# Hybrid decoder trunk on one core: the scan layer's cross product in rounded halves, its first tile's scaling issued earlier, and other PSUM banks for two products of the attention

## The chip, the cores and the metric

The kernel runs on one core of one Trainium2 chip. The metric is the device time of one execution in microseconds (us). TensorE (PE; PEld is its loading of the stationary operand) multiplies matrices into PSUM, VectorE (DVE) and ScalarE (ACT) work on tiles of 128 partitions, GpSimd (POOL) does small arithmetic and issues some DMAs, and SyncE (SP) issues the rest. Each engine takes its instructions in one fixed order, and semaphores make it wait for the others.

## The reference

The program is a decoder trunk of two layers on a sequence of 256 tokens with 1024 features, everything in float32. Each layer is a SwiGLU block, a mixer and a second SwiGLU block, each followed by a layer norm. The mixer of the first layer is a sparse attention: an indexer chooses 64 keys for each query, and 16 heads attend to them over a latent of 256 values. The mixer of the second layer is a state-space scan with 32 heads of 64 features in 4 groups. The parts that the change touches are these, cut from the reference:

```python
# attention: logits, softmax, and the values behind them (per head h)
p = softmax(einsum('bthr,btkr->bthk', q_abs, c_sel) * scale + mask)
o = einsum('bthr,hrd->bthd', einsum('bthk,btkr->bthr', p, c_sel), w_uv)

# scan: two chunks of 128 tokens; the second gets what the first left as its state
xdt = x * dt[..., None]
y_diag = einsum('bcgrls,bcsgrp->bclgrp', cb[:, :, :, None] * decay, xdt)
states = einsum('bclgn,bclgrp->bcgrpn', bm, xdt * decay_to_end[..., None])
y_off = einsum('bclgn,bcgrpn->bclgrp', cm, prev) * exp(a_cs_l)[..., None]
yz = (y_diag + y_off + x * d_skip) * silu(z)
yz = yz * rsqrt(mean(square(yz), -1) + eps)    # per group of 512 features
out = (yz * norm_g) @ w_out
```

For two chunks, `y_off` of the second chunk is (C of chunk 1, times B of chunk 0) applied to the first chunk's `xdt * decay_to_end`. The matrix C·B between the chunks is the "cross" of the kernel.

## The kernel before

**Products in halves.** A plain float32 matmul runs in two passes on the traced PE. Nearly all products of the kernel are done another way: each operand is split into a rounded part H (type float32r, written by a copy on ACT) and the rest L = x − H (a subtraction on DVE), and `mm3` (lines 538 to 541) issues three matmuls, H·H, H·L and L·H. Weights come as 128 x 1024 blocks over SP's DMA queue (`raw`), ACT makes `wh` from each (line 326, or 324 with a scale), DVE makes `wl` (lines 354 and 351), and for five blocks ACT writes −raw and a POOL DMA adds (lines 332 and 333). `W.pump` makes the next blocks' halves, ahead of their use.

**The order.** Every instruction is issued in the order of the Python code, and that order is the order on each engine; no scheduler changes it. Tiles live in rotating pools; of PSUM's eight banks, two are called `pmm`, two `ptr`, and four `acc00`, `acc01`, `acc10`, `acc11`. `pspare(n)` (line 453) deals out `pmm`, `pmm`, `acc00`, `acc01` (n = 2) in turn, by the counter `spare[0]`.

**The attention's stretch.** `logits(0, 1, 0)` computes 8 heads' logits of the first 128 queries into two spare banks; DVE adds the mask (line 1202) and ACT takes the exponentials (line 1213). Then `v_half` runs three times: two blocks' product on PE into a spare bank, and a copy to SBUF on ACT (line 1174). Then `out_both(0, 0)` multiplies the first block of the output weights into `acc00` and `acc01`.

**The scan's groups.** The loop at line 1676 handles four groups g of eight heads. The two chunks of tokens are called tiles 0 and 1. Between the group's own steps it puts pieces of other work, f[0] to f[7], to keep PE fed: for g = 0 and 1 projections of the next group (`xs_tile`: 24 matmuls on PE, then a convolution, one instruction on ACT at line 1497 and three on DVE at line 1500; `z_half`), for g = 2 the last projections in turn with pieces of the output product (`out_piece`), for g = 3 output pieces. The order in a group is: f[0]; `x_tok` (or, for g = 0, `decay_cb`); `x_end`, which makes `xe` on DVE; f[1]; f[2]; `diag(0)`, 8 small products on PE; `gate(0)` on DVE; `carry`, one float32 product of `cross` and `xe` on PE (line 1587) with two DVE steps; f[3]; `square(0)` on ACT (line 1597) and `root(0)` on POOL (lines 525 and 531); `diag(1)` and `gate(1)`; f[4]; `square(1)`, `root(1)`, then `norm(0)` on ACT (line 1603); f[5]; `y_tr(0)`, four transposes on PE of what `norm(0)` wrote (line 1608), split into halves `yH`, `yL`; and the same for tile 1. What `cross` holds is computed once, ahead of the loop (line 1522).

Of the kernel before, what the change touches and what calls it, by code (L numbers as in the profile page):

```python
# [11 lines left out]
F32 = mybir.dt.float32  # L12
F32R = mybir.dt.float32r
# [399 lines left out]
def trunk_kernel(ctx: ExitStack, tc: tile.TileContext, widths, forms, x, ln_g, ln_b, wts, kvg, convp,  # L413
                 dt_bias, a_log, d_skip, norm_g, out):
    nc = tc.nc
# [3 lines left out]
    wk = ctx.enter_context(tc.tile_pool(name="wk", bufs=1))  # L419
# [6 lines left out]
    def nm(s):  # L426
        cnt[0] += 1
        return f"{s}_{cnt[0]}"
# [4 lines left out]
    def f2(s):  # L433
        return wk.tile([128, 512], F32, name=nm(s), tag="f2", bufs=9)
# [4 lines left out]
    def r2(s):  # L439
        return wk.tile([128, 512], F32R, name=nm(s), tag="r2", bufs=10)  # L440

    def tiny(s, n=32):
        return wk.tile([128, n], F32, name=nm(s), tag=f"tiny{n}", bufs=14 if n == 32 else 4)
# [7 lines left out]
    spare = [0]  # L451

    def pspare(n):

        spare[0] = (spare[0] + 1) % (n + 2)
        if spare[0] < 2:
            return pmm()
        a, b = divmod(spare[0] - 2, 2)
        return psum.tile([128, 512], F32, name=nm("psp"), tag=f"acc{a}{b}", bufs=1)
# [74 lines left out]
    def split_psum(H, L, ps):  # L534
        nc.scalar.copy(H, ps)
        nc.vector.tensor_sub(L, ps, H.bitcast(F32))  # L536

    def mm3(ps, lh, ll, rh, rl, first, last, on=False):
        nc.tensor.matmul(ps, lh, rh, start=first, stop=False, skip_group_check=on)  # L539
        nc.tensor.matmul(ps, lh, rl, start=False, stop=False, skip_group_check=on)  # L540
        nc.tensor.matmul(ps, ll, rh, start=False, stop=last, skip_group_check=on)  # L541
# [474 lines left out]
    def attention(xT, u, ln_i):  # L1016
# [3 lines left out]
        lt, ki, qs, ss = {}, {}, {}, {}  # L1020
# [157 lines left out]
        oT, po, lgs, pTs = {}, {}, {}, {}  # L1178

        def pair_heads(t, hf, b):  # L1180
            return head_banks(8, 512 // (128 * (t + 1)), 8 * hf)[2 * b:2 * b + 2]

        def logits(t, hf, b, now=True):

            hss = pair_heads(t, hf, b)
            nk, per = 128 * (t + 1), len(hss[0])
            bank = pmm if t else lambda: pspare(2)
            ps = [bank(), bank()]
            for i in range(per):
                for q in range(2):  # L1190
                    h = hss[q][i]
                    p0, hp = (h % 2) * 64, h // 2
                    nc.tensor.matmul(ps[q][:, i * nk:(i + 1) * nk],
                                     qv[hp // 4][p0:p0 + 64, hp % 4, t * 128:(t + 1) * 128],
                                     kT[hp // 4][p0:p0 + 64, (hp % 4) * 256:(hp % 4) * 256 + nk],
                                     start=True, stop=True)
            mx = tiny("mx")
            lgs[t, hf, b] = lg = [f2("lg"), f2("lg")]
            for q in range(2):
                for i, h in enumerate(hss[q]):  # L1200
                    c = slice(i * nk, (i + 1) * nk)
                    nc.vector.tensor_tensor_reduce(out=lg[q][:, c], in0=ps[q][:, c], in1=mb[t][:, :nk],
                                                   scale=-(HD ** -0.5), scalar=3e38, op0=ALU.add, op1=ALU.min,
                                                   accum_out=mx[:, h:h + 1])
                if now:
                    exps(t, hss[q], lg[q], mx)
            return lambda: [exps(t, hss[q], lg[q], mx) for q in range(2)]

        def exps(t, hs, lg, mx):
            nk = 128 * (t + 1)  # L1210
            for i, h in enumerate(hs):
                c = slice(i * nk, (i + 1) * nk)
                nc.scalar.activation(lg[:, c], lg[:, c], AF.Exp, bias=mx[:, h:h + 1], scale=-1.0,
                                     accum_out=sums[t][:, h:h + 1])
# [22 lines left out]
        def pv(t, hf, b):  # L1237

            hss = pair_heads(t, hf, b)
            if not b:  # L1240
                po[t, hf] = psum.tile([128, 512], F32, name=nm("po"), tag=f"acc1{hf}", bufs=1)
            pT = pTs.pop((t, hf, b))
            for i in range(len(hss[0])):
                for kt in range(t + 1):
                    for q in range(2):
                        h = hss[q][i]
                        p0, j = (h % 2) * 64, h % 8 // 2
                        nc.tensor.matmul(po[t, hf][p0:p0 + 64, j * 128:(j + 1) * 128], v[kt][:, h * 64:(h + 1) * 64],
                                         pT[q][:, (i * (t + 1) + kt) * 128:(i * (t + 1) + kt + 1) * 128],
                                         start=kt == 0, stop=kt == t)  # L1250

        def o_split(t, hf):
            oT[t, hf] = (r2("oH"), r2("oL"))
            split_psum(*oT[t, hf], po[t, hf])
# [42 lines left out]
        k_pair(3)  # L1297
        pv(0, 0, 0)
        o_split(0, 0)
        logits(0, 1, 0)  # L1300
        for i in range(2):
            W.free(uk + i)
# [74 lines left out]
    def ssd(xT, u, ln_i):  # L1377
# [132 lines left out]
            W.pump(1 + i % 2)  # L1510

        cbm = f4("cbm")
        cross = f2("cross")

        def cb_cross():

            pt = pspare(4)
            for g in range(SG):
                c = slice(g * 256 + 128, g * 256 + 256)
                nc.tensor.matmul(pt[:, g * 128:(g + 1) * 128], bT[:, g * 256:g * 256 + 128], cTt[:, c],  # L1520
                                 start=True, stop=True)
            nc.scalar.copy(cross, pt)

        def cb(t):
            pt = pspare(4)
# [9 lines left out]
        def hv(ap):  # L1535
            return ap.rearrange("p (h d) -> p h d", h=8)

        def hb(ap, g):
            return ap[:, g * 8:(g + 1) * 8][:, :, None].to_broadcast([128, 8, 64])
# [13 lines left out]
                                 .to_broadcast([128, 8, 128]))  # L1553

        yT = {}
        y, xd, xe, ss = {}, {}, {}, {}

        def x_tok(t, g):

# [12 lines left out]
        def x_end(g):  # L1572
            xe[g] = f2("xe")
            nc.vector.tensor_mul(hv(xe[g]), hv(y[0]), hb(dend, g))

        def diag(t, g):
            m = M.pop((t, g))
# [6 lines left out]
        def carry(g):  # L1584

            po = ptr()
            nc.tensor.matmul(po, cross[:, g * 128:(g + 1) * 128], xe[g], start=True, stop=True)
            nc.vector.tensor_mul(hv(xe[g]), hv(po), hb(eacs, g))
            nc.vector.tensor_add(xd[1], xd[1], xe[g])

# [4 lines left out]
        def square(t):  # L1595
            ss[t] = tiny("ss")
            nc.scalar.activation(xd[t], y[t], AF.Square, accum_out=ss[t][:, 0:1])
# [4 lines left out]
        def norm(t):  # L1602
            nc.scalar.activation(y[t], y[t], AF.Copy, scale=ss[t])
# [72 lines left out]
        for g in range(SG):  # L1676
            if g < 2:
                f = [lambda i=i: xs_tile(g + 1, i, u + i) for i in range(4)]
                f += [lambda t=t, i=i: (z_half(g + 2, t, i, u + 4), W.pump(1)) for t in range(2) for i in range(2)]
            elif g == 2:  # L1680
                x3 = [lambda i=i: xs_tile(3, i, u + 2 * i) for i in range(4)]
                o0 = [lambda i=i: out_piece(i, u + 2 * i + 1) for i in range(4)]
                f = [x3[0], x3[1], o0[0], x3[2], o0[1], x3[3], o0[2], o0[3]]
            else:
                f = [lambda i=i: out_piece(4 + i, u + i) for i in range(6)]
            f[0]()
            if g:
                x_tok(0, g)
                x_tok(1, g)
            else:  # L1690
                decay_cb(0, 0)
                decay_cb(1, 0)
            x_end(g)
            f[1]()
            f[2]()
            py[0] = diag(0, g)
            gate(0, g, py[0])
            carry(g)
            if g < 3:
                decay_load(0, g + 1)  # L1700
            f[3]()
            square(0)
            root(0)
            py[1] = diag(1, g)
            gate(1, g, py[1])
            if g < 3:
                decay_load(1, g + 1)
            f[4]()
            square(1)
            root(1)  # L1710
            norm(0)
            if g < 3:
                decay_seg(0, g + 1)
            f[5]()
            y_tr(0, g)
            norm(1)
            if g < 3:
                decay_seg(1, g + 1)
                f[6]()
                flush()  # L1720
                y_tr(1, g)
                decay_exp(0, g + 1)
                decay_exp(1, g + 1)
                f[7]()
                decay_cb(0, g + 1)
                decay_cb(1, g + 1)
                W.lows()
                u += 8
# [19 lines left out]
    u, _ = ffn(xT, u, 5, last=True)  # L1748
# [36 lines left out]
```

## Time and profile before

| | us |
|---|---|
| median of 3 runs (lowest, highest) | 1011.57 (1011.35, 1012.05) |
| the profiled execution's own time | 1011.34 |
| its span from the first to the last instruction | 1009.6 |
| PE busy, sum of the records | 998.8 |
| DVE busy | 905.6 |
| ACT busy | 662.0 |
| POOL busy | 109.5 |

The execution that was profiled is one of its own; 1.7 us of its time lie outside the span. [...] A start is a start; an end of a matmul is modelled. The page's chain and its "idle before" name what an engine waited for last.

### The profile page before, as it was taken

The numbers are of one execution on the slowest core, as the hardware profiler recorded it, in microseconds if no ns is written. First come the engines' busy times: TensorE is split into PE (matmuls) and PEld (weight loads), VectorE is DVE, ScalarE is ACT, GpSimd is POOL, SyncE is SP. The second block draws the span as 40 slices with busy tenths as digits, with TensorE's granted clock in tenths as the row PEclk, the third lists the DMA queues.
The fourth block names the chain that finished last, engine by engine and source line by source line (L and its number), as shares of the span: only waits on it lengthen the run. The fifth ranks groups of instructions, "written<-read, shape, count | busy, mean of one in ns | idle before, by whom it ended". The sixth has DMA issues, their size and how long they took to land.

```text
span 1009.6 us, 14555 instructions
## 1 busy us (share of the span) xinstructions
PE 998.8 (99%) x5273; PEld 845.8 (84%) x5273; DVE 905.6 (90%) x1224; ACT 662.0 (66%) x968; POOL 109.5 (11%) x149
## 2 busy tenths in 40 slices
PE   9999999999999999999999999999999999999997
PEld 6888888898788888888888888999899888888886
DVE  6899999889898999999899998788999978899996
ACT  6676776476755777764576776486876645676670
POOL 0010110100000101100010110150221100010100
PEclk9999999999999999999999999999999999999999
DMA  9699889551654899995599989557765654699981
GB/s 346 221 289 282 241 260 344 181 172 59 232 181 127 272 275 239 264 376 202 126 276 271 248 264 359 172 171 248 220 211 182 243 188 136 169 261 288 289 254 42
DMA packets 66055, 231.69 MB, mean 229 GB/s; under 512 B 8112, under 2 KB 9136, under 8 KB 65984
## 3 DMA queue, kind: packets, MB, share of 16 engines
q1 hardware_dynamic: 54288, 189.84, 51.6%
q0 software_dynamic: 11120, 40.41, 21.7%
q8 instruction: 41, 0.67, 0.3%
q10 hardware_dynamic: 576, 0.52, 0.2%
q14 instruction: 30, 0.25, 0.1%
HBM read 193.48 MB, written 1.08 MB: 193 GB/s over the span
## 4 chain that ended last, share of the span: by engine, by line
PE 91%; DVE 5%; DMA 1%; ACT 1%; issue 1%; POOL 0%; ACTq 0%; DVEq 0%; POOLq 0%
PE pmm L539 13%; PE pmm L540 13%; PE pmm L541 13%; PE acc L539 10%; PE acc L541 10%; PE acc L540 10%; PE ptr L539 2%; PE ptr L541 2%; PE ptr L540 2%; PE pxs L539 2%; PE pxs L541 2%; PE pxs L540 2%; PE pmm L705 1%; DVE wl L354 1%; PE ptr L705 1%; PE ptr L795 1%
## 5 line engine op out<-in xcount | busy, mean ns | idle before, releaser
L354 DVE TENSOR_TENSOR wl<-raw,wh 128x1024 fp32r<-128x1024 f32 (+3 forms) x424 | 495.9, 1212 | 14.9 <-ACT wh L326 14.3
L326 ACT CAST wh<-raw 128x1024 fp32r<-128x1024 f32 (+2 forms) x431 | 429.0, 1043 | 97.0 <-DVE raw L293 47.3
L539 PE MATMUL acc<-wh,hH 128*128 128x512 f32 (+1 forms) x352 | 138.1, 392 | 0.0
L541 PE MATMUL acc<-wh,hL 128*128 128x512 f32 (+1 forms) x352 | 136.6, 388 | 0.0
L540 PE MATMUL acc<-wl,hH 128*128 128x512 f32 (+1 forms) x352 | 136.3, 387 | 0.0
L539 PE MATMUL pmm<-wh,xT 128*128 128x512 f32 (+2 forms) x304 | 119.1, 392 | 0.0
L541 PE MATMUL pmm<-wh,xT 128*128 128x512 f32 (+2 forms) x304 | 116.8, 384 | 0.0
L540 PE MATMUL pmm<-wl,xT 128*128 128x512 f32 (+2 forms) x304 | 116.7, 384 | 0.1
L266 POOL DMA_DIRECT2D raw<-raw x64 | 55.7, 875 | 490.6 <-DVE raw L293 260.5
L541 PE MATMUL pmm<-wh,xf 128*128 128x512 f32 x256 | 99.6, 389 | 0.0
L539 PE MATMUL pmm<-wh,xf 128*128 128x512 f32 x256 | 99.6, 389 | 0.0
L540 PE MATMUL pmm<-wl,xf 128*128 128x512 f32 x256 | 99.6, 389 | 0.0
L541 PEld LDWEIGHTS acc<-wh,hL 128*128 128x128 f32 x352 | 66.1, 188 | 13.8
L293 DVE TENSOR_TENSOR raw<-raw,raw 128x1024 f32<-128x1024 f32 x64 | 77.1, 1220 | 0.2
L540 PEld LDWEIGHTS acc<-wl,hH 128*128 128x128 f32 x352 | 66.2, 188 | 12.9
L539 PEld LDWEIGHTS acc<-wh,hH 128*128 128x128 f32 x352 | 66.1, 188 | 12.9
L541 PEld LDWEIGHTS pmm<-wh,xT 128*128 128x128 f32 x304 | 57.0, 188 | 11.8 <-DVE xT L536 0.4
L540 PEld LDWEIGHTS pmm<-wl,xT 128*128 128x128 f32 x304 | 57.2, 188 | 10.9 <-DVE wl L354 0.8
L539 PEld LDWEIGHTS pmm<-wh,xT 128*128 128x128 f32 x304 | 57.1, 188 | 9.9
L541 PEld LDWEIGHTS pmm<-wh,xf 128*128 128x128 f32 x256 | 48.1, 188 | 10.0
L539 PEld LDWEIGHTS pmm<-wh,xf 128*128 128x128 f32 x256 | 48.0, 188 | 10.0
L540 PEld LDWEIGHTS pmm<-wl,xf 128*128 128x128 f32 x256 | 48.0, 188 | 9.9
(321 smaller groups left out, 1783.6 us busy)
## 6 DMA issues: line engine op xcount, KB each, us to landing
raw<-in_wts_dram SPq DMA_DIRECT2D x338, 512.0 KB, 5.7
raw<-raw POOLq DMA_DIRECT2D x64, 512.0 KB, 6.1
M<-scr POOLq DMA_DIRECT2D x8, 512.0 KB, 5.4
lng<-in_ln_g_dram SPq DMA_DIRECT2D x6, 512.0 KB, 5.6
lnb<-in_ln_b_dram SPq DMA_DIRECT2D x6, 512.0 KB, 5.3
wl<-raw POOLq DMA_DIRECT2D x5, 512.0 KB, 5.5
raw<-in_wts_dram SPq DMA_DIRECT2D x4, 408.0 KB, 4.7
out_dram<-x SPq DMA_DIRECT2D x4, 256.0 KB, 2.0
```

The costliest lines, as they stand in the source:

```text
L266: self.nc.gpsimd.dma_start(self.raw[r], self.raw[other], accum_op=ALU.add)
L293: self.nc.vector.tensor_add(self.raw[r], self.raw[r], self.raw[other])
L326: nc.scalar.copy(h[:, c:c + n], raw[:, c:c + n])
L354: self.nc.vector.tensor_sub(lo[:, s], raw[:, s], h[:, s].bitcast(F32))
L539: nc.tensor.matmul(ps, lh, rh, start=first, stop=False, skip_group_check=on)
L540: nc.tensor.matmul(ps, lh, rl, start=False, stop=False, skip_group_check=on)
L541: nc.tensor.matmul(ps, ll, rh, start=False, stop=last, skip_group_check=on)
L705: nc.tensor.matmul(ps, H[:, k * 128:(k + 1) * 128], xT.HL[:, k, :], start=k == 0, stop=False)
L795: nc.tensor.transpose(v[:, i, t * 128:(t + 1) * 128], hs[t][:, i * 128:(i + 1) * 128], ident)
```

## The change

There are three edits.

1. In the attention, `spare[0] = 3` ahead of `logits(0, 1, 0)`. Its two banks become `pmm`, `pmm` (they were `acc00`, `acc01`), and the three halves of v go to `acc00`, `acc01`, `pmm` (they went to `pmm`, `pmm`, `acc00`).
2. In the scan, `cross` is kept as H and L (`split_psum`: the same copy on ACT, now to float32r, and a subtraction on DVE). `x_end` gets a copy of `xe` to float32r, `xeH`, on ACT. The new `x_low`, called after f[1], makes `xeL` on DVE. `carry` calls `mm3` in place of the one float32 product.
3. In the scan's loop `norm(0)` is issued ahead of `square(1)` and `root(1)`.

```diff
@@ attention @@
         pv(0, 0, 0)
         o_split(0, 0)
+        spare[0] = 3
         logits(0, 1, 0)
@@ ssd @@
         cbm = f4("cbm")
-        cross = f2("cross")
+        cross = [wk.tile([128, 512], F32R, name=nm("cross"), tag="f2", bufs=9) for _ in range(2)]
...
-            nc.scalar.copy(cross, pt)
+            split_psum(*cross, pt)
...
-        y, xd, xe, ss = {}, {}, {}, {}
+        y, xd, xe, xeH, xeL, ss = {}, {}, {}, {}, {}, {}
...
         def x_end(g):
             xe[g] = f2("xe")
             nc.vector.tensor_mul(hv(xe[g]), hv(y[0]), hb(dend, g))
+            xeH[g] = wk.tile([128, 512], F32R, name=nm("xeH"), tag="f2", bufs=9)
+            nc.scalar.copy(xeH[g], xe[g])
+
+        def x_low(g):
+            xeL[g] = wk.tile([128, 512], F32R, name=nm("xeL"), tag="f2", bufs=9)
+            nc.vector.tensor_sub(xeL[g], xe[g], xeH[g].bitcast(F32))
...
         def carry(g):
             po = ptr()
-            nc.tensor.matmul(po, cross[:, g * 128:(g + 1) * 128], xe[g], start=True, stop=True)
+            c = slice(g * 128, (g + 1) * 128)
+            mm3(po, cross[0][:, c], cross[1][:, c], xeH[g], xeL[g], True, True)
             nc.vector.tensor_mul(hv(xe[g]), hv(po), hb(eacs, g))
             nc.vector.tensor_add(xd[1], xd[1], xe[g])
@@ the loop over g @@
             x_end(g)
             f[1]()
+            x_low(g)
             f[2]()
...
             f[4]()
+            norm(0)
             square(1)
             root(1)
-            norm(0)
```

**ACT's order in group 0, around `x_end`.** `cv` is the convolution's first step (the line 1497 of before is 1498 after), `wh` and `wl` are weight halves, and the next rows down belong to f[1]. Before:

```order
L332 ACTIVATE wl_7041<-raw_6871 128x1024
L1497 ACTIVATE cv_7075<-pxs_7049,convp_sb 128x256
L1492 ACT_TABLE_LOAD
L1492 ACTIVATE xsT_7034<-cv_7035 128x256
L326 CAST wh_7083<-raw_6927 128x1024
L1497 ACTIVATE cv_7112<-pxs_7086,convp_sb 128x256
```

and after the change:

```order
L332 ACTIVATE wl_7043<-raw_6872 128x1024
L1577 CAST xeH_7051<-xe_7049 128x512
L1498 ACTIVATE cv_7079<-pxs_7053,convp_sb 128x256
L1493 ACT_TABLE_LOAD
L1493 ACTIVATE xsT_7036<-cv_7037 128x256
L326 CAST wh_7087<-raw_6929 128x1024
L1498 ACTIVATE cv_7118<-pxs_7092,convp_sb 128x256
```

The copy to `xeH` stands ahead of f[1]'s convolution step; it waits for DVE's `xe`.

**DVE's order in group 2, from `xe` to `gate(0)`.** The rows `cv` are f[1]'s convolution (128x255, 254 and 253), and `xdt` at the end is `gate(0)`. Before:

```order
L1574 TENSOR_TENSOR xe_7682<-xdt_7669,dend_6237 128x512
L1500 SCALAR_TENSOR_TENSOR cv_7710<-pmm_7684,convp_sb,cv_7710 128x255
L1500 SCALAR_TENSOR_TENSOR cv_7710<-pmm_7684,convp_sb,cv_7710 128x254
L1500 SCALAR_TENSOR_TENSOR cv_7710<-pmm_7684,convp_sb,cv_7710 128x253
L351 SCALAR_TENSOR_TENSOR wl_7662<-raw_7559,ng_sb,wh_7661 128x1024
L351 SCALAR_TENSOR_TENSOR wl_7720<-raw_7589,ng_sb,wh_7719 128x1024
L1592 TENSOR_TENSOR xdt_7669<-ptr_7744,xtok_7670 128x512
```

and after the change:

```order
L1575 TENSOR_TENSOR xe_7696<-xdt_7683,dend_6237 128x512
L1501 SCALAR_TENSOR_TENSOR cv_7726<-pmm_7700,convp_sb,cv_7726 128x255
L1501 SCALAR_TENSOR_TENSOR cv_7726<-pmm_7700,convp_sb,cv_7726 128x254
L1501 SCALAR_TENSOR_TENSOR cv_7726<-pmm_7700,convp_sb,cv_7726 128x253
L351 SCALAR_TENSOR_TENSOR wl_7676<-raw_7573,ng_sb,wh_7675 128x1024
L1581 TENSOR_TENSOR xeL_7738<-xe_7696,xeH_7698 128x512
L351 SCALAR_TENSOR_TENSOR wl_7736<-raw_7603,ng_sb,wh_7735 128x1024
L1600 TENSOR_TENSOR xdt_7683<-ptr_7762,xtok_7684 128x512
```

`xeL` stands behind f[1]'s convolution, and in this group behind a weight half too. In groups 0 and 1 it stands directly behind the convolution's three rows, and in group 3, which has no convolution, behind one `wl`.

**ACT's order in group 0, around `norm(0)`.** `xtok` is written by `square`, `xdt` by `norm`. Before:

```order
L332 ACTIVATE wl_7215<-raw_7081 128x1024
L1597 ACTIVATE xtok_7000,ss_7219<-xdt_6999 128x512
L1603 ACTIVATE xdt_6990<-xdt_6990,rs_7183 128x512
L1478 ACTIVATE zs_7239<-pmm_7198 128x512
```

and after the change:

```order
L332 ACTIVATE wl_7223<-raw_7085 128x1024
L1611 ACTIVATE xdt_6992<-xdt_6992,rs_7191 128x512
L1605 ACTIVATE xtok_7002,ss_7228<-xdt_7001 128x512
L1479 ACTIVATE zs_7247<-pmm_7206 128x512
```

`norm(0)` no longer stands behind `square(1)`, which waits for DVE's `gate(1)`. The other groups change in the same way. POOL and SP keep their order.

## The prediction

> **What bounds the kernel now.** I read the page's busy times and its chain first, then the scan's stretches, then what PE waited for, and last the order of time around each edited step.
>
> ```profile
> PE 998.8 (99%) x5273; PEld 845.8 (84%) x5273; DVE 905.6 (90%) x1224; ACT 662.0 (66%) x968; POOL 109.5 (11%) x149
> PE 91%; DVE 5%; DMA 1%; ACT 1%; issue 1%; POOL 0%; ACTq 0%; DVEq 0%; POOLq 0%
> 711.00:740.00 29.00, 28.48 (x193) 25.66 (x192) 25.82 (x38) 23.63 (x34) 5.49 (x8) 1.00 0.78 227
> 740.00:770.00 30.00, 30.00 (x194) 26.59 (x193) 27.35 (x39) 21.37 (x30) 4.66 (x6) 1.00 0.60 198
> 770.00:800.00 30.00, 30.00 (x177) 25.83 (x176) 29.18 (x36) 18.74 (x26) 3.15 (x5) 1.00 0.70 234
> PE acc L539 <- ACT v L1174: 0.9, 1, 0.9
> PE ptr L1608 <- ACT xdt L1603: 0.5, 1, 0.5
> ```
>
> The first row gives busy time by engine, the second the chain that ended last. The next three are stretches of the scan's loop: the columns are the length, then busy time (count) of PE, PEld, DVE, ACT and POOL, then PE's granted clock and the DMA. PE is without a gap for 60 us from 740. So a wait that PE gets here is paid in full, since hardly any later idle time is there to give it back. DVE is busy 29.18 of 30 us near the end, so it has little room. The last two rows are PE's own waits at two places of the change: the copies of v, and `norm(0)`'s output.
>
> **The change part by part.**
>
> *The carry on PE.* A float32 product takes two passes, 0.91 us together. Three matmuls of 512 columns at the 0.23 us pitch seen below (722.07 to 722.29 to the next) take 0.69. Four groups would gain 0.22 us each, if nothing waits. But PE now waits for two new steps, `xeH` on ACT and `xeL` on DVE. The rows are group 0's `xe` on DVE, the next step on ACT (f[1]'s convolution), the carry on PE and its cost on the chain; then the prices.
>
> ```profile
> 710.56 0.69 DVE L1574 TENSOR_TENSOR xe<-xdt,dend 128x512 f32<-128x512 f32 x1
> 708.62 0.55 ACT L1497 ACTIVATE cv<-pxs,convp_sb 128x256 f32<-128x256 f32 x1
> 711.47 1.08 PE L1587 MATMUL ptr<-xe,cross 128*128 128x512 f32 x2
> 741.00 0.91 PE ptr L1587 x2
> 691.61 0.59 ACT L1522 COPY cross<-pmm 128x512 f32<-128x512 f32 x1 [0.88 <-PE pmm L1520]
> 695.08 1.52 DVE L1500 SCALAR_TENSOR_TENSOR cv<-pxs,convp_sb,cv 128x255 f32<-128x255 f32 x3 [2.18 <-ACT cv L1497]
> L536 DVE TENSOR_TENSOR yL<-ptr,yH 128x512 fp32r<-128x512 f32 x8 | 5.5, 689 | 5.0 <-ACT yH L535 5.0
> 245.50 1.04 ACT L1174 COPY v<-pmm 128x512 f32<-128x512 f32 x2
> 247.08 0.19 PEld L539 LDWEIGHTS acc<-wh,oH 128*128 128x128 f32 x1 [1.29 <-ACT v L1174]
> 247.19 0.19 PEld L540 LDWEIGHTS acc<-wl,oH 128*128 128x128 f32 x1
> ```
>
> `xe` ends at 710.56 + 0.69 = 711.25. ACT was free at 708.62 and did f[1]'s convolution step then. Now the copy to `xeH` stands ahead of it and waits for `xe`: ACT stands still for 2.6 us, and behind it queue the convolution step, a table load and a weight half. DVE's convolution queues behind ACT's step, and `xeL` behind that. So the chain from the end of `xe` is: 0.03 to ACT; the copy, 0.48 to the next start (two copies of v start within 1.04 - 0.57); the convolution step, 0.56 to its end; 0.03 to DVE; three steps on DVE, 1.52 less the 0.09 by which records overlap, 1.43; `xeL`, 0.69. That is 3.22 us. The trace has no copy of this kind from SBUF; the nearest rows are the 0.59 above and half of a weight's 1.04, so the chain is good to 0.1. PE starts 0.06 later, needs 0.11 for the load in front (247.08 to 247.19), and has two of the three matmuls left, 0.46, the first having run on `xeH` alone.
>
> Group 0: `xeL` at 714.47, the carry over at 715.10, before 711.47 + 0.91 = 712.38: PE loses 2.72 us.
>
> ```profile
> 738.81 0.69 DVE L1574 TENSOR_TENSOR xe<-xdt,dend 128x512 f32<-128x512 f32 x1
> 736.43 0.57 ACT L1497 ACTIVATE cv<-pxs,convp_sb 128x256 f32<-128x256 f32 x1 [0.25 <-PE pxs L541]
> 740.84 1.08 PE L1587 MATMUL ptr<-xe,cross 128*128 128x512 f32 x2
> 767.88 0.69 DVE L1574 TENSOR_TENSOR xe<-xdt,dend 128x512 f32<-128x512 f32 x1
> 765.11 0.56 ACT L1497 ACTIVATE cv<-pmm,convp_sb 128x256 f32<-128x256 f32 x1 [0.79 <-PE pmm L541]
> 769.91 2.48 DVE L351 SCALAR_TENSOR_TENSOR wl<-raw,ng_sb,wh 128x1024 fp32r<-128x1024 f32 x2
> 769.41 1.08 PE L1587 MATMUL ptr<-xe,cross 128*128 128x512 f32 x2
> 794.63 0.69 DVE L1574 TENSOR_TENSOR xe<-xdt,dend 128x512 f32<-128x512 f32 x1
> 795.23 2.48 DVE L351 SCALAR_TENSOR_TENSOR wl<-raw,ng_sb,wh 128x1024 fp32r<-128x1024 f32 x2
> 797.95 1.08 PE L1587 MATMUL ptr<-xe,cross 128*128 128x512 f32 x2
> ```
>
> These are groups 1, 2 and 3 (three, four and three rows). Group 1: `xe` ends at 739.50, `xeL` at 742.72, the carry at 742.72 + 0.06 + 0.57 = 743.35 instead of 741.75: 1.60 lost. Group 2: the order has a weight half between the convolution and `xeL`, 1.20 more (two in 2.48): from 768.57 to 772.99, the carry over at 773.62 instead of 770.32: 3.30 lost. Group 3 has no convolution in f[1]. `xeH` is done at 795.32 + 0.03 + 0.59 = 795.94, and `xeL` follows one weight half, 796.43 to 797.12, ahead of PE's 797.95: nothing is lost, 0.22 gained. Together 2.72 + 1.60 + 3.30 - 0.22 = 7.40 us. After a stall PE, ACT and DVE are late by about the same amount, as f[2]'s convolution, `gate(0)` and `square(0)` stand behind the same rows, so the next group meets the same alignment.
>
> The other new steps cost nothing: `cross`'s copy takes the place of one of the same size, and its subtraction, 0.69 on DVE, falls into the 2.18 us for which DVE waits at 695 (without that cover it would cost at most 0.69, ahead of f[0]). In the groups DVE gets 0.6 each, inside the time that it now waits for ACT.
>
> *`norm(0)` ahead of `square(1)`.*
>
> ```profile
> 718.72 1.06 ACT L332 ACTIVATE wl<-raw 128x1024 fp32r<-128x1024 f32 x1
> 721.80 0.63 ACT L1597 ACTIVATE xtok<-xdt 128x512 f32<-128x512 f32 x1 [2.03 <-DVE xdt L1593]
> 722.43 0.71 ACT L1603 ACTIVATE xdt<-xdt,rs 128x512 f32<-128x512 f32 x1
> 718.24 0.57 POOL L531 TENSOR_TENSOR rs<-rse,mhalf 128x1 f32<-128x1 f32 x1
> 722.07 0.39 PE L540 MATMUL pmm<-wl,xT 128*128 128x512 f32 x1
> 722.29 0.39 PE L541 MATMUL pmm<-wh,xT 128*128 128x512 f32 x1
> 723.20 0.66 PE L1608 MATMUL ptr<-ident,xdt 128*128 128x128 f32 x4 [0.52 <-ACT xdt L1603]
> ```
>
> In group 0 PE is ready at 722.29 + 0.23 = 722.52 and starts the transposes at 723.20, because `norm(0)` stood behind `square(1)`. Its factor `rs` is there at 718.81 and ACT is free at 719.78, so it will be done some 2 us before PE asks: 0.68 gained. In the other groups PE shows no wait there, so nothing. `square(1)` starts no later, since ACT idled 2.03 us in front of it.
>
> *The banks of v.*
>
> ```profile
> 246.45 0.58 ACT L1174 COPY v<-psp 128x512 f32<-128x512 f32 x1
> 245.83 0.39 PE L541 MATMUL psp<-wh,cT 128*128 128x512 f32 x1
> 247.08 0.50 PE L539 MATMUL acc<-wh,oH 128*128 128x512 f32 x1 [0.86 <-ACT v L1174]
> 246.82 1.66 DVE L1224 TENSOR_SCALAR lg<-lg,rsum 128x128 f32<-128x128 f32 x8
> 248.57 1.04 PE L1232 MATMUL ptr<-ident,lg 128*128 128x128 f32 x8
> ```
>
> PE is ready for `out_both` at 246.06 and waits for the third copy of v, which empties `acc00`. With the change the first copy empties it, at 245.50 + 0.57 = 246.07, and the second `acc01` at 246.54, 0.4 ahead of need; the third bank is `pmm`, asked for later. PE starts at 246.13, 0.95 earlier. Of that not all lasts: the next transposes need DVE's eight scalings, the last done at 248.48, so PE is through at 248.65 instead of 249.44, 0.79 earlier. I take 0.70, with 0 and 0.95 as the ends.
>
> *Sum:* +7.40 - 0.68 - 0.70 = +6.0 us. The profiled execution, 1011.34, becomes 1017.4. It lies 0.23 under the median of the runs, 1011.57, which becomes 1017.6.
>
> **The rivals.**
>
> *The clock drops in the long stall.* In group 2 PE idles from 769.64 (its first matmul done) to 773.05, 3.4 us, longer than any pause in the rows above, where the clock reads 1.00 throughout. If the granted clock halved afterwards, the next tile of 24 matmuls would run at twice its pitch:
>
> ```profile
> 770.49 0.12 PE pmm L539
> ```
>
> 24 x 0.12 = 2.9 us more, so 1020.5. For it speaks only the length of the stall; against it, that it is one stall and group 0's is shorter (2.4). [...]
>
> *Only the first stall counts.* Once PE is 2.72 us late, ACT and DVE could use that time to get ahead, and `xeL` of groups 1 and 2 would be ready. Then 2.72 - 3 x 0.22 - 0.68 - 0.70 = +0.7, 1012.3. For it: PE is the busiest engine, and DVE follows it. Against: all that DVE and ACT do next stands behind the same late rows, and the lead would have to be 2 to 4 us.
>
> *Faster: the carry never waits.* If `xeL` were ready before PE asks in every group, as the rows give for group 3 (0.8 us ahead), the three gains stay: 4 x 0.22 + 0.68 + 0.70 = 2.3, 1009.3. It is decided by one comparison a group: the end of `xeL` against the end of `diag(0)`. It would need DVE to make `xe` 3.1, 1.9 and 3.6 us earlier than in the rows of groups 0, 1 and 2, or ACT not to hold its order. Nothing in the profile speaks for that outside group 3.
>
> **How the numbers follow.** The forecast, three stalls, gets 0.72, with a range of its own of 1016 to 1019.5: the attention's ends (0.7 up, 0.3 down), 0.1 a link in three chains of several links. The clock gets 0.11, the single stall 0.10, the faster case 0.05; 0.02 is for more than these. The predicted time is 1017.6. The range 1014.8 to 1020.8 takes in the forecast and the clock and leaves out the single stall and the faster case. What can be told from no change is 0.2%, 2 us: faster 0.05, same 0.10, slower 0.85.
>
> **What would show it.** In the new profile PE should wait at the carry (second matmul) on DVE's `xeL` in groups 0, 1 and 2, longest in group 2 and not at all in group 3, and the copy `xeH` should show ACT idle for some 2 to 4 us on DVE's `xe`. The wait of PE at line 1608 of before on ACT in group 0 and the 0.9 us on v should be gone. The clock should read 1.00 after the stalls. The forecast is wrong if `xeL` ends before `diag(0)` in groups 0 to 2, or if the waits are there and the span does not grow with them.

## The result and the profile after

The changed kernel takes 1025.21 us, the median of 4 runs (1020.85 to 1026.78), against 1011.46 (1011.26 to 1012.05) for the kernel before on the same chip: 1.0128 times as long, 95% interval 1.0096 to 1.0160. It is slower, as forecast, but by 13.75 us where 6.0 were forecast, and outside the range. Its runs lie up to 6 us apart, those of the kernel before 0.8. The profiled execution took 1025.73 us, with a span of 1024.0 (before 1009.6).

First the page's busy times; then what PE waited for from 600 us to the end (total, times, longest); then stretches of the scan's loop with the columns of the prediction's windows, cut where the granted clock changes.

```profile
PE 1005.4 (98%) x5277; PEld 852.5 (83%) x5277; DVE 908.4 (89%) x1229; ACT 663.8 (65%) x972; POOL 110.3 (11%) x149
```

```profile
PE ptr L540 <- DVE xeL L1581: 7.4, 3, 3.2
PE ptr L539 <- ACT xeH L1577: 1.0, 2, 0.6
PE acc L539 <- DVE xtok L1571: 0.4, 1, 0.4
```

```profile
712.50:719.00 6.50, 5.05 (x21) 4.86 (x22) 5.34 (x10) 3.61 (x6) 0.00 (x0) 0.50 0.60 182
719.25:746.25 27.00, 25.97 (x174) 23.43 (x173) 20.05 (x27) 20.06 (x30) 6.13 (x8) 1.00 0.72 202
746.50:753.00 6.50, 5.03 (x21) 4.84 (x22) 6.32 (x11) 2.31 (x4) 0.00 (x0) 0.50 0.49 158
753.25:783.75 30.50, 26.84 (x168) 23.53 (x167) 24.17 (x31) 20.45 (x29) 4.24 (x6) 1.00 0.48 157
784.00:787.25 3.25, 3.25 (x17) 3.25 (x16) 2.58 (x4) 0.00 (x0) 0.00 (x0) 0.50 0.54 160
```

Three waits of PE for `xeL` are there, 7.4 us together, in groups 0, 1 and 2 and not in group 3; the waits on v and on `norm(0)` are gone. But PE is 6.6 us *busier* than before, though the float32 carry's 0.91 us a group became 0.69. The third column from the right in the windows says why: after each of the three waits the granted clock is 0.50, for some 6.8, 6.8 and 3.4 us. There the matmuls of 256 columns follow each other at 0.21 us, and at 0.12 once the clock reads 1.00 again (starts at 717.96, 718.17 and 718.38, then 719.19, 719.31 and 719.43). So about half of PE's work in those rows, 5.05 + 5.03 + 3.25 = 13.3 us, is time that it would not take at the full clock: 6.7 us, an estimate from these pitches.

To place the rest I time a group by the starts of `diag(0)` and `diag(1)` on PE. These are the rows of `diag` in the changed kernel's timeline, two a group (start, duration):

```profile
709.05 1.97 PE L1587 MATMUL ptr<-xdt,M 128*128 128x64 f32 x16
719.66 1.89 PE L1587 MATMUL py<-xdt,M 128*128 128x64 f32 x16
742.82 1.90 PE L1587 MATMUL ptr<-xdt,M 128*128 128x64 f32 x16
753.74 1.90 PE L1587 MATMUL py<-xdt,M 128*128 128x64 f32 x16
777.47 1.90 PE L1587 MATMUL ptr<-xdt,M 128*128 128x64 f32 x16
787.79 1.90 PE L1587 MATMUL ptr<-xdt,M 128*128 128x64 f32 x16
810.80 1.89 PE L1587 MATMUL ptr<-xdt,M 128*128 128x64 f32 x16
816.03 1.89 PE L1587 MATMUL ptr<-xdt,M 128*128 128x64 f32 x16
```

(Before, the same starts are 709.66 and 715.25, 739.11 and 744.62, 767.68 and 773.20, 796.22 and 801.63.)

| from diag(0) to diag(1) | before | forecast adds | after adds | over the forecast |
|---|---|---|---|---|
| group 0 | 5.59 | 2.72 | 5.02 | 2.30 |
| group 1 | 5.51 | 1.60 | 5.41 | 3.81 |
| group 2 | 5.52 | 3.30 | 4.80 | 1.50 |
| group 3 | 5.41 | -0.22 | -0.18 | 0.04 |

From the first `diag(0)` to the last transposes (`y_tr(1)` of group 3, 813.46 before and 827.88 after) the loop takes 103.80 us before and 118.83 after: +15.03, where 7.40 - 0.68 = 6.72 were forecast. Ahead of the loop the first `diag` starts 0.61 us earlier than before. So the attention is as forecast, and all that was missed, 8.3 us, lies in groups 0 to 2: 7.6 in the table, and 0.67 between group 2's `x_tok` and its `diag(0)`, 7.19 us for 6.52.

### The profile page after: what moved, and what is told of

Same layout as the page of the kernel before. It is cut to its first block, busy times and chain, and to the rows that moved or that the text cites. A ratio compares the mean times of both kernels' runs of the same rounds, so it can differ in the third digit from the quotient of the medians.

```text
span 1024.0 us, 14567 instructions
## 1 busy us (share of the span) xinstructions
PE 1005.4 (98%) x5277; PEld 852.5 (83%) x5277; DVE 908.4 (89%) x1229; ACT 663.8 (65%) x972; POOL 110.3 (11%) x149
## 4 chain that ended last, share of the span: by engine, by line
PE 88%; DVE 6%; DMA 3%; ACT 1%; issue 1%; POOL 1%; DVEq 0%; ACTq 0%; SPq 0%; POOLq 0%
PE pmm L541 12%; PE pmm L540 12%; PE pmm L539 12%; PE acc L539 10%; PE acc L541 9%; PE acc L540 9%; PE ptr L540 2%; PE ptr L541 2%; PE ptr L539 2%; DMA M<-scr 2%; DVE wl L354 1%; PE pmm L705 1%; PE pxs L539 1%; PE ptr L705 1%; PE pxs L540 1%; PE pxs L541 1%
## 5 line engine op out<-in xcount | busy, mean ns | idle before, releaser
L354 DVE TENSOR_TENSOR wl<-raw,wh 128x1024 fp32r<-128x1024 f32 (+3 forms) x424 | 495.1, 1209 | 13.7 <-ACT wh L326 13.3
```

Source lines behind the costliest of these rows:

```text
L354: self.nc.vector.tensor_sub(lo[:, s], raw[:, s], h[:, s].bitcast(F32))
```

## The experiments

The theory: the three waits cost what was forecast; on top comes the clock, which halves after each of them, 6.7 us, and a follow-on of it, decay tiles that are loaded late, with the rest. The rival: the split's extra instructions on DVE and ACT hold PE up, or the other two edits do, and the clock only follows. The table has the medians, the ratio to the kernel before on the same chip with its 95% interval, and the loop as defined above in the profiled execution.

| kernel | us | ratio (interval) | loop, us | over before |
|---|---|---|---|---|
| changed | 1025.21 | 1.0128 (1.0096 to 1.0160) | 118.83 | 15.03 |
| split alone | 1027.48 | 1.0147 (1.0130 to 1.0164) | 120.21 | 16.41 |
| banks and norm alone | 1010.46 | 0.9986 (0.9977 to 0.9995) | 103.47 | -0.33 |
| changed + 11, 11, 14 matmuls | 1019.29 | 1.0076 (1.0061 to 1.0091) | 112.30 | 8.50 |
| changed + 11, 11, 14 narrow matmuls | 1020.08 | 1.0081 (1.0066 to 1.0096) | 111.32 | 7.52 |
| changed + 5, 5, 7 matmuls | 1017.84 | 1.0063 (1.0046 to 1.0080) | 110.76 | 6.96 |
| changed + 3, 3, 3 matmuls | 1019.56 | 1.0079 (1.0057 to 1.0102) | 112.29 | 8.49 |
| changed + earlier load | 1023.53 | 1.0115 (1.0100 to 1.0131) | 116.09 | 12.29 |
| changed + 11, 9, 14 matmuls + earlier load | 1018.43 | 1.0066 (1.0052 to 1.0080) | 110.97 | 7.17 |
| changed + 7, 5, 10 matmuls + earlier load, xeH behind f[1] | 1014.87 | 1.0030 (1.0019 to 1.0041) | 107.60 | 3.80 |
| xeH on DVE | 1012.29 | 1.0002 (0.9993 to 1.0011) | 105.22 | 1.42 |
| carry behind f[3] | 1012.51 | 1.0009 (1.0000 to 1.0019) | 105.17 | 1.37 |
| carry behind f[3], xeL ahead of f[2] | 1011.13 | 0.9992 (0.9984 to 1.0001) | 103.76 | -0.04 |

**Which edit costs.** The split alone:

```diff
-        spare[0] = 3
         logits(0, 1, 0)
...
-            norm(0)
             square(1)
             root(1)
+            norm(0)
```

> Only the split of the carry is left of the change; the banks of v and the norm's place are as before. Theory (the split brings waits of PE at the carry, and the granted clock halves after them): all of the loss is here, 1025.2 + 0.7 + 0.6 = 1026.5 us, between 1022 and 1029, since the changed kernel's own runs spread over 6 us; the clock falls below 1.00 at three places of the scan's loop. Rival (part of the loss belongs to the other two edits, for instance since the early norm stands ahead of other work on ACT): under 1020.

And the other two edits without it (the kernel before with `spare[0] = 3` and `norm(0)` moved):

> The other two edits alone, with the carry as one float32 product. Theory: nothing waits longer than before, the two gains stay, 1011.5 - 0.6 - 0.7 = 1010.2 us, clock 1.00 in the scan. Rival: these edits bring part of the loss, 1013 or more.

1027.48 and 1010.46 us. All of the loss belongs to the split; without it the change is a gain of 0.14% (0.05 to 0.23). That is the only version here that is faster than both kernels by its interval. In its trace PE waits for nothing at either of the two places; the first `diag` starts 0.74 us earlier than before, and from `diag(1)` of group 0 to the transposes it is 7.28 us for 7.95. Of this 0.67 the loop keeps 0.33: 0.34 goes again between group 2's `x_tok` and its `diag(0)` (6.86 us for 6.52), behind a wait of DVE for a decay tile (see the late loads below).

**Is it the clock?** PE is kept busy through the waits, and nothing else is taken away:

```diff
+            for _ in range((11, 11, 14, 0)[g]):
+                nc.tensor.matmul(po, xT.HL[:, 0, :128], xT.HL[:, 0, :], start=True, stop=True)
             mm3(po, cross[0][:, c], cross[1][:, c], xeH[g], xeL[g], True, True)
```

> The changed kernel with 11, 11 and 14 extra matmuls (a slice of the projections' input times itself, 128x512, 0.23 us each, 2.5 to 3.2 us) ahead of the carry of groups 0, 1 and 2, into the carry's own bank, whose first real matmul overwrites them. They fill PE's idle time and take away none of its waits. Theory: after the stalls PE ran at half rate for 5.2, 5.3 and 3.4 us of work, which cost half of that, 6.9 us; with PE kept busy the clock stays at 1.00 and the time falls to 1025.2 - 6.9 = 1018.3, to 1017.5 if the late loads of the decay go too, near the forecast of 1017.6; the spread between runs goes. Rival (the loss is in DVE's and ACT's extra work and order, the clock only follows): no gain, 1025 to 1027, since the matmuls take nothing off DVE.

1019.29 us: 36 more matmuls make the kernel 5.9 us faster, and the clock reads 1.00 from the start of the loop to its end. The waits were not shortened, so the rival falls: DVE and ACT have the same work as in the changed kernel. 1.0 us more is left than the 1018.3 expected. In this kernel's waits stands a row on DVE, and behind it one on PE:

```profile
DVE M L1545 <- DMA M<-scr: 2.6, 1, 2.6
PE acc L539 <- DVE xtok L1571: 0.8, 1, 0.8
```

With fewer of the same matmuls (5, 5 and 7) most of the waiting stays:

> As e_warm, but with 5, 5 and 7 extra matmuls for 11, 11 and 14: 1.2 to 1.6 us of the 2.6 to 3.4 us of waiting are filled, PE's waits for xeL stay at 1 to 2 us. All changes of the clock in the traces so far stand on a raster of 3.413 us, and the intervals of it that ended in a drop held 1.1 to 2.6 us of PE's work. Theory (the gate judges each interval of 3.4 us by how much of it PE worked): the filled share is enough, clock 1.00, 1019.3 as e_warm or up to 0.5 less, since nothing outlasts the wait. Rival (a pause of over 1 us halves the clock wherever it lies): the clock halves in some groups, 1021 or more.

1017.84 us, clock 1.00 in the loop, and no wait for M on DVE. It is 1.0 us under the lowest time expected, 1018.8, since no decay tile is late and nothing outlasts the wait. This is the kernel of the forecast: the change at full clock. Its row in the waits, and its rows of `diag` from `diag(1)` of group 0 on:

```profile
PE ptr L540 <- DVE xeL L1581: 3.7, 3, 1.6
```

```profile
717.39 1.90 PE L1587 MATMUL py<-xdt,M 128*128 128x64 f32 x16
740.55 1.90 PE L1587 MATMUL ptr<-xdt,M 128*128 128x64 f32 x16
747.88 1.89 PE L1587 MATMUL py<-xdt,M 128*128 128x64 f32 x16
770.93 1.90 PE L1587 MATMUL ptr<-xdt,M 128*128 128x64 f32 x16
779.75 1.90 PE L1587 MATMUL ptr<-xdt,M 128*128 128x64 f32 x16
802.73 1.89 PE L1587 MATMUL ptr<-xdt,M 128*128 128x64 f32 x16
807.97 1.89 PE L1587 MATMUL ptr<-xdt,M 128*128 128x64 f32 x16
```

The first `diag(0)` starts at 709.03 here. The groups add 2.77, 1.82, 3.30 and -0.17 us to those of before, against the forecast's 2.72, 1.60, 3.30 and -0.22, and `norm(0)` gives 0.68 in group 0 (from `diag(1)` to the transposes 7.27 us, before 7.95).

**The late loads.** POOL issues the load of the next group's second decay tile behind `root(0)`, and `root(0)` waits for `square(0)` on ACT, which stands behind f[3]'s convolution there, which waits for PE's f[3]. In the changed kernel f[3] of group 0 runs at half rate, and the load goes out at 723.78 us. Pieces of the changed kernel's chain, two in group 0 and one in group 1 (start, duration; a load's goes from its issue to its landing), then from its timeline ACT's convolution step for f[3] and DVE's first use of the tile in groups 0 and 1:

```profile
722.38 0.78 POOL rse L525
...
723.78 8.86 DMA M<-scr
...
757.84 8.45 DMA M<-scr
```

```profile
719.86 0.56 ACT L1498 ACTIVATE cv<-pxs,convp_sb 128x256 f32<-128x256 f32 x1 [3.74 <-PE pxs L541]
...
732.74 1.23 DVE L1545 CUSTOM_DVE_ANT_1 M<-M,nacs 128x1024 f32<-128x1024 f32 x1 [2.88 <-DMA M<-scr]
...
766.31 1.23 DVE L1545 CUSTOM_DVE_ANT_1 M<-M,nacs 128x1024 f32<-128x1024 f32 x1 [2.26 <-DMA M<-scr]
```

Before, that load was issued at 718.77 and DVE did not wait for it. Now DVE loses 2.9 and 2.3 us, so `xe` of the next groups comes later.

That the half rate is the cause is not shown. DVE asks for the tile 6.1 us after its issue in group 0 (6.9 before) and 6.2 us after it in group 1 (5.7 before). But the loads took 8.9 and 8.5 us to land; before, they were issued at 718.77 and 749.14 and landed at 723.93 and 754.76, after 5.2 and 5.6 us. And group 1's wait comes at full clock too: 2.6 us with 11, 11 and 14 matmuls (its row is shown above), and 1.9 with banks and norm alone:

```profile
DVE M L1545 <- DMA M<-scr: 1.9, 1, 1.9
```

Why a load lands sooner or later is open. What the wait in group 1 costs PE can be read off: 0.34, 0.67 and 0.99 us between group 2's `x_tok` and its `diag(0)` for waits of 1.94, 2.26 and 2.58 us (banks and norm alone, changed, changed + 11, 11, 14), that is, all beyond 1.6 us. The narrow matmuls' wait of 0.99 costs nothing there.

The edit moves the load ahead, once in the changed kernel and once with the extra matmuls (11, 9, 14):

```diff
-            root(0)
             py[1] = diag(1, g)
-            gate(1, g, py[1])
             if g < 3:
                 decay_load(1, g + 1)
+            root(0)
+            gate(1, g, py[1])
```

> The changed kernel with one edit: the load of the next group's second decay tile is issued by POOL ahead of root(0). No extra matmuls, so the clock still halves. Theory (the late loads are a follow-on of the half rate, and add their own wait): DVE's waits for M of 2.9 and 2.3 us go, groups 1 and 2 lose up to 1.5 us less; 1023.5, in 1021 to 1025. Rival (the loads are hidden behind the half rate): 1025 as the changed kernel.

> As e_warm, with two edits: group 1 gets 9 extra matmuls for 11, since they outlasted the wait by 0.5 us there, and the load of the next group's second decay tile is issued by POOL ahead of root(0) and not behind it. Theory (the forecast's sum left out only the clock and these late loads): DVE's waits for M (2.6 us in e_warm's groups) go, so does PE's 0.8 on xtok; 1019.3 - 0.5 - 0.8 = 1018.0, the forecast of 1017.6 within 0.5. Rival (the loads were late but hid): 1018.8 to 1019.3.

1023.53 and 1018.43 us, and DVE's wait for M is gone in both; in the first, group 2's `diag(0)` comes 6.52 us after its `x_tok` again. The first is 1.7 us under the changed kernel's median, within that kernel's own spread; its loop is 2.7 us shorter, with 13.65 us of half rate in it for 17.07, so part of the 2.7 is the clock's. I do not split it, and that the time hits the 1023.5 expected is in part luck. The second is 0.9 us under the kernel with 11, 11 and 14; the two intervals overlap, but the loop is shorter by 1.3, as expected (0.5 + 0.8).

**How the wait is made.** The copy `xeH`, taken out of `x_end` into `x_high`, stands behind f[1]'s convolution step on ACT; all else is as in the last kernel, with 7, 5 and 10 extra matmuls for the shorter waits:

```diff
             x_end(g)
             f[1]()
+            x_high(g)
             x_low(g)
             f[2]()
```

> As e_warm_mload, but the copy xeH is issued behind f[1]'s convolution step on ACT and not ahead of it; carry and xeL stand where the change has them; 7, 5 and 10 extra matmuls for the shorter waits. Theory (of the carry's wait, the part that the order on ACT makes is the head of the queue: f[1]'s convolution step and DVE's three behind it start only after xe): DVE's idle 1.15 us ahead of that convolution goes in groups 0 to 2, each wait is about 1.1 us shorter, 1018.4 - 3.3 = 1015.1, clock 1.00. Rival (the wait is DVE's work itself, xe, three convolution steps and xeL in a row): 1017.5 to 1018.5.

1014.87 us, 3.6 less. DVE's rows in group 0, in the changed kernel (two) and here (three):

```profile
709.95 0.68 DVE L1575 TENSOR_TENSOR xe<-xdt,dend 128x512 f32<-128x512 f32 x1
711.78 1.51 DVE L1501 SCALAR_TENSOR_TENSOR cv<-pxs,convp_sb,cv 128x255 f32<-128x255 f32 x3 [1.15 <-ACT cv L1498]
```

```profile
709.86 0.69 DVE L1575 TENSOR_TENSOR xe<-xdt,dend 128x512 f32<-128x512 f32 x1
710.46 1.51 DVE L1501 SCALAR_TENSOR_TENSOR cv<-pxs,convp_sb,cv 128x255 f32<-128x255 f32 x3
711.89 0.68 DVE L1583 TENSOR_TENSOR xeL<-xe,xeH 128x512 fp32r<-128x512 f32 x1
```

DVE's 1.15 us of idle time is gone: over a third of each wait was ACT standing still for `xe` with other work behind it. The rest is DVE's own order, as the next kernel shows, where `xeH` is made on DVE directly behind `xe`, and `xeL` behind that (`nc.vector.tensor_copy` for `nc.scalar.copy`, and no f[1] between):

> The changed kernel with xeH made on DVE directly behind xe, and xeL behind that, so ACT's queue is as before and the split is two DVE steps, about 1.2 us, at the same place. PE's wait shrinks from 2.6, 2.6 and 3.4 us to about 0.7, 0.1 and 0.3. Theory (a short wait leaves the clock alone): 1010.5 + 1.1 - 0.9 = 1010.7, with DVE's extra 1.2 us a group up to 1012; clock 1.00. Rival (any wait behind diag halves the clock for 6.8 us): 2.6 more for the first group alone, 1013.3 or more.

1012.29 us, the same as before within the interval, above the 1010.7 expected at best and 0.3 above the 1012 expected at most. PE's waits for the two halves are 0.2 us each, and the clock stays up, but one of 0.8 has come in behind `gate(0)`, since DVE has two steps more ahead of it:

```profile
PE ptr L1585 <- DVE xdt L1598: 0.8, 1, 0.8
PE ptr L540 <- DVE xeL L1579: 0.2, 1, 0.2
```

**Can the split pay?** The carry moves behind f[3], `xeH` behind f[1] and `xeL` behind f[2]:

```diff
             f[1]()
-            x_low(g)
+            x_high(g)
             f[2]()
+            x_low(g)
...
-            carry(g)
             if g < 3:
                 decay_load(0, g + 1)
             f[3]()
+            carry(g)
```

> The same split with the same instructions, but the copy xeH is issued behind f[1], the subtraction xeL behind f[2], and the carry behind f[3], so that ACT does not stand still for xe and PE asks for the carry 24 matmuls later (2.9 us). Theory: no wait at the carry, the clock stays up, the split gives 4 x 0.22: 1011.5 - 0.9 - 0.6 - 0.7 = 1009.3, at most 1010.5. Rival (the extra instructions on DVE and ACT cost time wherever they stand): 4 x 0.6 us on each, with DVE busy 29 of 30 us in group 2: 1012 to 1016.

1012.51: not the 1009.3 expected, but within the rival's 1012 to 1016. PE still waits for `xeL`, since DVE does f[2]'s convolution and a weight half first (the row of the waits, and two of DVE in group 0):

```profile
PE ptr L540 <- DVE xeL L1583: 1.8, 3, 1.4
```

```profile
714.48 1.21 DVE L354 TENSOR_TENSOR wl<-raw,wh 128x1024 fp32r<-128x1024 f32 x1
715.62 0.68 DVE L1583 TENSOR_TENSOR xeL<-xe,xeH 128x512 fp32r<-128x512 f32 x1
```

So `xeL` goes ahead of f[2] (`x_high(g)`, `x_low(g)`, then `f[2]()`):

> As e_late (xeH behind f[1], carry behind f[3]), but the subtraction xeL stands ahead of f[2], so that on DVE neither f[2]'s convolution nor the weight half behind it is ahead of it. In e_late's profile xeL began at 715.62 behind those two, and PE waited 1.4, 0.2 and 0.3 us for it. Theory (the loss of a split carry is only the order in which its copies stand): xeL now begins at about 712.9 of group 0, 1.7 us ahead of the carry, no wait in any group, 1010.5 - 4 x 0.22 = 1009.6 us, at most 1010.5. Rival (DVE's and ACT's extra instructions cost time wherever they stand): 1011.5 to 1013, as e_late.

1011.13, 1.5 above the 1009.6 expected and 0.4 under the rival's 1011.5 to 1013. No wait at the carry is left. From `diag(0)` to `diag(1)` groups 0, 1 and 3 gain 0.16, 0.16 and 0.18 us on the kernel with banks and norm alone, the split's whole gain. But two new waits have come in, in group 2 for `gate(0)` and in group 0 for `norm(1)`, whose input is late since the carry's DVE steps now stand behind f[3]:

```profile
PE ptr L1589 <- DVE xdt L1602: 0.4, 1, 0.4
PE ptr L1618 <- ACT xdt L1613: 0.4, 1, 0.4
```

That is 0.8 lost for 0.5 gained, and the loop is 0.3 us longer than with banks and norm alone. The rival's point stands here in a weaker form: with DVE busy 29 of 30 us in group 2, a step more on it shows up somewhere.

**What the clock goes by.** The extra matmuls once more, but 64 columns wide and in float32, as in `diag`: `nc.tensor.matmul(po[:, :64], ident, ident[:, :64], ...)`, 11, 11 and 14 of them.

> As e_warm, but the extra matmuls are float32 of 128x64 (the identity's columns), of the kind and size that diag issues, 11, 11 and 14 at 2 x 0.11 us, so PE is busy for the same time with an eighth of the columns. Theory A (the gate goes by whether PE is busy): clock 1.00, 1019.3 as e_warm. Theory B (the gate goes by how much the array does, and diag's small matmuls count for little, which is why it fell less than 1 us into the wait): the clock still halves in most of the three groups, 1024 to 1027.

1020.08 us, clock 1.00 in the loop: theory B, as put there, falls. With the narrow matmuls PE is busy for 3.21 to 3.41 us of every interval of the loop, and no drop followed. That leaves how much is enough, and 3 wide ones a group were tried last:

> As e_half_fill, with 3 extra matmuls in each of groups 0 to 2 (0.7 us). In the twelve kernels traced so far, weigh each interval of the 3.413 us raster by the columns that PE streamed in it, at the pitch of the wide matmuls (0.23 us for 512 columns, float32 ones counted twice): the nine intervals that ended in a drop have 0.17 to 0.34, all others 0.40 or more. Theory (the gate goes by that share of an interval, not by the length of a pause): in groups 0 and 1 the remaining 1.9 us of wait leave 0.4 or more, no drop; in group 2, with 2.7 us left, it depends on where the raster lies; 1018 us without a drop there and 1020 with one, and each drop seen has a share below 0.40, each interval without one above 0.34. Rival (a pause of about 2 us halves the clock): drops in groups 0, 1 and 2, 1023 or more.

1019.56 us, and in the profiled execution one drop, in group 2 alone, as the theory has it; the drops in groups 0 and 1 that the rival needs did not come. Its four runs fit a drop or none: 1019.39, 1019.72 and 1022.75 us with a mean granted clock of 0.996, and 1017.90 with 0.999; but 1022.75 is more than one drop explains. The profiled execution's windows, cut in steps of 3.413 us (see the last section): one in group 0, two in group 2.

```profile
712.29:715.71 3.42, 1.62 (x11) 1.54 (x12) 2.30 (x6) 3.41 (x6) 0.00 (x0) 1.00 0.95 298
773.73:777.15 3.42, 0.90 (x4) 0.58 (x4) 3.38 (x5) 1.74 (x2) 0.00 (x0) 1.00 0.44 153
777.15:780.56 3.41, 3.41 (x18) 3.41 (x17) 3.06 (x5) 0.00 (x0) 0.00 (x0) 0.50 0.48 151
```

PE was idle for 1.8 us of the first, and the clock stayed up; the second, with 0.90 us of work, was followed by half rate.

## Why the prediction was right or wrong

**Right: the place, the chain and the price of the waits.** PE waits at the carry's second matmul for `xeL` in groups 0, 1 and 2, and not in group 3; `xeH` finds ACT idle for 2.6 us in group 0. The chain was to end with `xeL` at 714.47, less the 0.61 by which the loop began earlier, so 713.86; the row has 713.22 + 0.68 = 713.90, and PE at 713.95. With the clock up (the kernel with 5, 5 and 7) the four terms are 7.72 for 7.40, the norm 0.68 for 0.68, the start 0.63 for 0.70, and the median 1017.84 for 1017.6.

```profile
710.67 0.62 ACT L1577 CAST xeH<-xe 128x512 fp32r<-128x512 f32 x1 [2.56 <-DVE xe L1575]
713.22 0.68 DVE L1581 TENSOR_TENSOR xeL<-xe,xeH 128x512 fp32r<-128x512 f32 x1
711.34 0.50 PE L539 MATMUL ptr<-xeH,cross 128*128 128x512 f32 x1 [0.32 <-ACT xeH L1577]
713.95 0.79 PE L540 MATMUL ptr<-xeL,cross 128*128 128x512 f32 x1 [2.11 <-DVE xeL L1581]
```

**Wrong: "The clock should read 1.00 after the stalls."** This is the step that failed: the sum had no term for the clock. The rival of the halved clock had been confined to group 2, as the longest pause, 3.4 us, at 2.9 us for one tile. It came in all three groups, at 6.7 us in all. Group 0's drop is the telling one: it came at 712.29, before PE had been idle for 1 us in one piece. The matmul behind the wait, 0.79 us in the row above, takes 0.50 in the kernel with 5, 5 and 7. By the estimate that is fitted to the runs in the last section, the drops go with the interval around the wait and not with the pause alone, and there `diag` weighs little: its sixteen records of 64 columns fill 1.9 us and are weighed as 0.9, and the wait stands right behind them. These rows were at hand; that columns may count was not.

**Wrong: "the next group meets the same alignment".** It does at full clock (1.82 for 1.60 and 3.30 for 3.30). In the changed kernel DVE waited 2.9 and 2.3 us for decay tiles, whose load POOL issues behind `root(0)`, and fell back against PE. The sum had no term for this either, and why the tiles were late is open, as said above. By difference it is the rest of the 8.3 us, about 1.6 beside the clock's 6.7: 0.67 ahead of group 2's `diag(0)`, where PE waits for `xtok`, and some 1.3 in group 1 (3.81 less half of 5.03; 0.2 of it is there at full clock too), while groups 0 and 2 together stay 0.4 under half of their busy time.

**A size.** The split gains 0.16 to 0.18 us a group, not 0.22; it changes nothing in the sum.

**The rivals.** That only the first stall counts is refuted by the waits in groups 1 and 2; that the carry never waits, by all three. That of the clock named what came, at two fifths of its price (2.9 us for 6.7), and its chance was too low: "the length of the stall" was the only thing I asked about.

## What to carry to other kernels

A wait on TensorE can cost more than its length: here three waits behind `diag`, 7.4 us together, were followed by half rate, which cost an estimated 6.7 us more. By the rule fitted to these runs, add up the columns that are streamed within some 3.4 us around the wait, not only the pause. Before an operand is split in two for a faster matmul, look at what its copies wait for in the order of their engines; here the copy at the head of ACT's queue, which waited 2.56 us for DVE, left DVE idle for 1.15 us ahead of its own next step. And where a wait can't be removed, a few matmuls whose result is overwritten may be worth more than they cost: 17 of them took 7.4 us off here, a part of it since no decay tile was late there.

## What the runs showed of the hardware

**When the clock changed.** Windows of 0.25 us on PE alone (length, busy time, granted clock, DMA share, GB/s) around three changes in group 0 and 1 of the changed kernel:

```profile
712.25:712.50 0.25, 0.00 (x0) 0.57 1.42 147
719.00:719.25 0.25, 0.25 (x4) 0.77 1.01 311
746.25:746.50 0.25, 0.00 (x0) 0.84 1.07 442
```

A mean of 0.57 between 1.00 and 0.50 puts the drop at 712.29; the other two are at 719.12 and 746.42. The half rate lasts 6.83 us in group 0, from drop to drop it is 34.13 us, and the stretch in group 2, from 783.97 to 787.38, lasts 3.41. So 3.413 us, a tenth of the 34.13, is taken as the step of a raster. Cut by it, the loop reads 0.50 or 1.00 in every interval, and nothing between, in all four of the fourteen kernels' profiles that have half rate there (changed, split alone, earlier load, 3 matmuls). Its place differs from one profile to the next: the first drop is at 712.29, 713.88 and 713.03 us in the first three. The 6 us between runs of the changed kernel go with the clock: 0.989, 0.989, 0.991 and 0.994 on the mean for 1025.73, 1026.78, 1024.69 and 1020.85 us. How much of a wait and of `diag` fell into one interval in each of these runs is not shown, as they have no windows of their own.

**What the intervals held.** Here are the four intervals of the changed kernel around its waits. The first two and the last ended in a drop, the third did not.

```profile
708.87:712.29 3.42, 2.58 (x18) 2.05 (x17) 2.25 (x4) 1.60 (x3) 0.99 (x2) 1.00 0.80 132
743.01:746.42 3.41, 2.21 (x17) 1.75 (x15) 2.22 (x5) 1.73 (x4) 0.00 (x0) 1.00 1.02 225
777.14:780.55 3.41, 2.51 (x20) 2.11 (x18) 2.19 (x6) 2.17 (x4) 0.00 (x0) 1.00 0.11 30
780.55:783.97 3.42, 1.11 (x7) 1.02 (x8) 3.42 (x5) 1.29 (x2) 0.00 (x0) 1.00 0.41 145
```

PE's busy time does not order them: a drop followed on 2.58 us, and none on 2.51 or, in the kernel with 3 matmuls, on 1.62. The ten intervals that ended in a drop held 0.69 to 2.58 us of it. In these runs the columns order them. Weigh each record by its columns at the wide matmuls' pitch (0.23 us for 512), those of float32 products twice, as the two records of the float32 carry took 0.91 us: `diag`'s 1.9 us are then 0.9. By this estimate the intervals that ended in a drop, ten in four kernels, hold 0.17 to 0.34 of full work, and every other interval of the loop in the fourteen profiles at full clock 0.40 or more (the third row above is the lowest). The kernel with 3 matmuls was forecast by it and came out so. It is a rule fitted to these runs, and it says nothing of other data or sizes; that the clock goes by columns is not shown. Each stretch of half rate in the loop ended with an interval that PE filled, 3.34 to 3.41 us.
